# Attention scores: two heads side by side in the halves of TensorE's rows, three matmuls of 64 rows each in place of two stacked ones of 128

## The chip, the cores and the metric

The kernel runs on one core of a Trainium2 chip. The metric is the device time of one execution in microseconds (us); lower is better. Below, TensorE is PE in the rows of the profile, its weight loads are PEld, VectorE is DVE, ScalarE is ACT, GpSimd is POOL and SyncE, which issues most transfers, is SP.

## The reference

The program is one layer of a decoder trunk on a sequence of 1,024 tokens of width 1,024: a norm, a wide projection, two token mixers, their merge and an output projection, a gated MLP with a short convolution, and a final norm. The change touches only the scores of the two mixers, that is the products of queries with keys before the softmax:

```python
# differential attention: 4 heads, each with two maps c = 0, 1 of width d = 64
s = jnp.einsum('bqhcd,bshcd->bhcqs', q_blk, k, preferred_element_type=jnp.float32) * scale
logits = s - slopes[:, None, None, None] * dist.astype(jnp.float32)
p = jax.nn.softmax(logits, axis=-1)
a = p[:, :, 0] - lam * p[:, :, 1]
...
# sliding window of 128: 8 query heads of width 64, two key heads, each shared by 4 query heads
s = jnp.einsum('bnqkgd,bnskd->bnkgqs', qb, kw, preferred_element_type=jnp.float32) * (d ** -0.5)
```

Both sum over 64 elements, half of the 128 rows that the other matmuls of this kernel use.

## The kernel before

All products are made at single precision out of two parts of a shortened float format: a number x is split into a high part xh (rounded by ScalarE) and a low part xl = x - xh (by VectorE). A product of two such numbers is normally three matmuls, high by high, high by low and low by high, added up in PSUM; low by low is left out.

The stages follow each other: `project` (the wide projection; queries and keys are stored to `qd` in memory as two parts, each as 64 rows per head, two heads in 128 rows), `attention`, `rest` (gates, merge, output projection), `hidden` and `down` (the MLP).

`attention` runs six units. Units 0 to 3 are the heads of differential attention, in steps of 128 queries (`da_step`): step i has queries i*128 to i*128+127 and keys up to (i+1)*128, so widths 128 to 1,024, in pieces ("cuts") of up to 512 columns; the first step takes 256 columns. For both maps c there are scores in a tile `sc` of the pool `psS` (two buffers), one VectorE instruction that adds the bias and finds the row's extreme (line 637, called the reduction below), one exponential on ScalarE (L638); then the two maps are combined (L643), transposed on TensorE (L649), split, and multiplied with the values in `da_av` (L661 to L663). Units 4 and 5 are the key heads of the window attention, in eight steps each (`sw_step`): four query heads, 256 columns each, scores at L721, reductions at L728, transposes at L742, the product with the values at L752.

Scores before the change are made by stacking: `q_stacks` loads the high part of one head's queries into 64 rows and the low part into the other 64 rows; `k_stack` loads the same 64 rows of the keys twice, once into each half, as one tile for the high part and one for the low part. A matmul over 128 rows then gives (qh + ql) * kh at once, a second one (qh + ql) * kl. So each head and cut has two matmuls of 128 rows, with all four terms.

The work that fills gaps in the attention stage is `back_half` (the columns of the wide projection for the gates, L160 to L162, matmuls of 512 columns), dealt out over the steps by the table `HALVES`. The order of instructions on each engine is decided when the program is built: a scheduler takes instructions by priority as their inputs come due, and each engine then runs its own list strictly as listed. `high_priority`, `issue_after` and `add_manual_dep` bend that order. A pool's `bufs` says how many tiles of one tag live at once; the parts for the scores are tiles of tag "u", eleven buffers.

Of the kernel before, what the change touches and what calls it, by code (L numbers as in the profile page):

```python
# [10 lines left out]
F32 = mybir.dt.float32  # L11
F32R = mybir.dt.float32r
AF = mybir.ActivationFunctionType
ALU = mybir.AluOpType
# [3 lines left out]
P = 128  # L18
D = 1024
T = 1024  # L20
# [20 lines left out]
C_NM, C_NF, C_NO, C_CB, C_CW, C_SUB, C_QS, C_SINK, C_LAM = 0, 8, 16, 24, 68, 200, 201, 205, 213  # L41
NVEC = C_LAM + 256


class Trunk:
    def __init__(self, tc, ins, out):
        self.tc, self.nc = tc, tc.nc
        (self.xT, self.w_in, self.w_br, self.w_mix, self.w_up, self.w_dn,
         self.vecs_d, self.bias_d) = ins
        self.out = out  # L50
        self.uid = 0
        self.stores = []
        self.uw = None
        self.front = None
        self.hs, self.defer, self.late = {}, [], []

    def name(self, s):
# [430 lines left out]
    def attention(self):  # L488
        nc, tc = self.nc, self.tc
        with ExitStack() as ctx:  # L490
            e = ctx.enter_context
            self.ap = e(tc.tile_pool(name="ap", bufs=1, side="right", reuse_waits="tile"))
            self.fpool = e(tc.tile_pool(name="fyp", bufs=1, side="right", reuse_waits="tile"))
            ap = self.ap

            lt = self.tl(self.gpool, [P, 64], "g", bufs=2)
            ls = self.st.tile([P, 4], F32, name="ls")
            for c in range(2):
                a = C_LAM + 128 * c
                nc.vector.tensor_tensor(lt, self.vecs[:, a:a + 64], self.vecs[:, a + 64:a + 128], ALU.mult)  # L500
                nc.vector.tensor_reduce(ls[:, c:c + 1], lt, axis=mybir.AxisListType.X, op=ALU.add)
            nc.scalar.activation(ls[:, 2:4], ls[:, 0:2], AF.Exp)
            self.neglam = self.cp.tile([P, 1], F32, name="neglam")
            nc.vector.tensor_tensor(self.neglam, ls[:, 3:4], ls[:, 2:3], ALU.subtract)
            nc.vector.tensor_scalar(self.neglam, self.neglam, LAM_INIT, None, ALU.subtract)
            self.nsink = self.cp.tile([P, 8], F32, name="nsink")
            nc.vector.tensor_scalar(self.nsink, self.vecs[:, C_SINK:C_SINK + 8], -1.0, None, ALU.mult)
            self.subw = self.cp.tile([P, 1], F32, name="subw")
            nc.vector.tensor_scalar(self.subw, self.vecs[:, C_SUB:C_SUB + 1], 1.0 - LAM_INIT, None, ALU.mult)

            self.bias = ap.tile([P, T + 256], F32, name="bias")
            nc.sync.dma_start(self.bias, self.bias_d)

            later = []
            st = self.q_stacks(0), self.kv_stacks(0)
            for b in self.back[0][0]:
                self.back_half(*b)
            for u in range(6):
                if st is None:
                    st = self.q_stacks(u), self.kv_stacks(u)  # L520
                if u < 4:
                    self.v_parts(u)
                elif u == 4:
                    self.sw_v(self.v32(17))
                y = self.tl(self.fpool, [P, T], "y", bufs=2) if u < 4 else None
                aT = None
                for i in range(NB):
                    if u < 4:
                        if i == 0:
                            self.s0 = self.tl(self.st, [P, NB], "s0", bufs=2)  # L530
                        if i % 2 == 0:
                            aT = self.da_at(i // 2)
                        self.da_step(u, i, st, aT)
                        if i % 2 == 1:
                            self.da_av(u, i // 2, aT, y)
                    else:
                        self.sw_step(u - 4, i, st)
                    for b in self.back[u + 1][i]:
                        self.back_half(*b)
                    self.flush(1)  # L540
                    if later:
                        later.pop(0)()
                st = None
                if u < 4:
                    later = self.da_norm(u, y)
            self.flush(0)
# [17 lines left out]

    def q_stacks(self, u):

        r = []
        for m in ((u,), (12, 13), (14, 15))[max(u - 3, 0)]:
            for c in range(2):
                a, b = slice(c * 64, c * 64 + 64), slice(64 - c * 64, 128 - c * 64)  # L570
                s = self.tl(self.ap, [P, T], "u", F32R, bufs=11)
                for part, to in enumerate((a, b)):
                    self.nc.sync.dma_start(s[to].bitcast(F32), self.qd[m, part, a])
                r.append(s)
        return r

    def k_stack(self, m, c):
# [7 lines left out]
        return r  # L585

    def kv_stacks(self, u):
        return [self.k_stack(4 + u, c) for c in range(2)] if u < 4 else self.k_stack(16, u - 4)

    def v32(self, m):  # L590
        v = self.tl(self.fpool, [P, T], "f", bufs=2)
# [27 lines left out]
    def da_step(self, h, i, st, aT):  # L619
        nc, ap = self.nc, self.ap  # L620
        q, k = st
        slope = 4.0 ** -(h + 1)
        w = (i + 1) * P

        lo = P if w == 640 else 0
        cuts = ((0, 256),) if i == 0 else ((0, w),) if w <= H2 else ((0, H2 - lo), (H2 - lo, w))
        pr = []
        for c in range(2):
            sc = self.tl(self.psS, [P, T], "sc")
            qs = q[c][:, i * P:(i + 1) * P]  # L630
            for part in range(2):
                for n0, n1 in cuts:
                    nc.tensor.matmul(sc[:, lo + n0:lo + n1], qs, k[c][part][:, n0:n1], start=part == 0, stop=part == 1)  # L633
            L = self.tl(ap, [P, T], "L", bufs=4)
            s = self.tl(self.st, [P, 4], "sm", bufs=8)
            o = 896 - i * P
            nc.vector.tensor_tensor_reduce(L[:, :w], sc[:, lo:lo + w], self.bias[:, o:o + w], slope, 3e38, ALU.add, ALU.min, s[:, 0:1])  # L637
            nc.scalar.activation(L[:, :w], L[:, :w], AF.Exp, bias=s[:, 0:1], scale=-1.0, accum_out=s[:, 1:2] if c else self.s0[:, i:i + 1])  # L638
            pr.append(L)

        nc.vector.reciprocal(s[:, 2:3], s[:, 1:2])
        nc.vector.tensor_scalar(s[:, 3:4], self.s0[:, i:i + 1], s[:, 2:3], self.neglam, ALU.mult, ALU.mult)
        nc.vector.scalar_tensor_tensor(pr[0][:, :w], pr[1][:, :w], s[:, 3:4], pr[0][:, :w], ALU.mult, ALU.add)  # L643
        qo = (i % 2) * P
        for j0 in range(0, i + 1, 4):
            nj = min(4, i + 1 - j0)
            ps = self.tl(self.psT, [P, 4, P], "t")
            for j in range(nj):
                nc.tensor.transpose(ps[:, j, :], pr[0][:, (j0 + j) * P:(j0 + j + 1) * P], self.ident)  # L649
            hi, lo = aT[j0 // 4, 0], aT[j0 // 4, 1]  # L650
            nc.scalar.copy(hi[:, :nj, qo:qo + P], ps[:, :nj, :])
            nc.vector.tensor_tensor(lo[:, :nj, qo:qo + P], ps[:, :nj, :], hi[:, :nj, qo:qo + P].bitcast(F32), ALU.subtract)
# [57 lines left out]
    def sw_step(self, g, n, st):  # L710
        nc, ap = self.nc, self.ap
        q, k = st
        k0 = max(n - 1, 0) * P
        w = P if n == 0 else 256
        bo = T + (P if n == 0 else 0)
        sc = self.tl(self.psS, [P, 4, 256], "sc")
        s = self.tl(self.st, [P, 4, 4], "sw", bufs=4)
        L = self.tl(ap, [P, 4, 256], "L", bufs=4)
        for h in range(4):
            for part in range(2):  # L720
                nc.tensor.matmul(sc[:, h, :], q[h][:, n * P:(n + 1) * P], k[part][:, k0:k0 + 256], start=part == 0, stop=part == 1)  # L721


        a, at, we = (0, w, w + 1) if n == 0 else (1, 0, w)
        nc.gpsimd.tensor_copy(L[:, :, at:at + 1], self.nsink[:, 4 * g:4 * g + 4].unsqueeze(2))
        for h in range(4):
            slope, ns = 2.0 ** -(4 * g + h + 1), self.nsink[:, 4 * g + h:4 * g + h + 1]
            nc.vector.tensor_tensor_reduce(L[:, h, a:w], sc[:, h, a:w], self.bias[:, bo + a:bo + w], slope, ns, ALU.add, ALU.min, s[:, 0, h:h + 1])  # L728
        for h in range(4):
            nc.scalar.activation(L[:, h, :we], L[:, h, :we], AF.Exp, bias=s[:, 0, h:h + 1], scale=-1.0, accum_out=s[:, 2, h:h + 1])  # L730
# [5 lines left out]
        po = self.tl(self.psT, [P, H2], "t")  # L736
        nblk = w // P
        parts = []
        for b in range(nblk):
# [4 lines left out]
            hi, lo = pt[:, 0], pt[:, 1]  # L744
# [7 lines left out]
                nc.tensor.matmul(po, va, pt, start=b == 0 and m == 0, stop=b == nblk - 1 and m == 1)  # L752
        t = self.tl(self.gpool, [P, 4, P], "g", bufs=2)[0:64]
        nc.scalar.copy(t, po[64:128].rearrange("p (h q) -> p h q", h=4))
        pv = po[0:64].rearrange("p (c e q) -> p c e q", c=2, e=2)
        tv = t.rearrange("p (c e) q -> p c e q", e=2)
        y = self.tl(ap, [P, 2, P], "ys", bufs=3)
        for e in range(2):
            nc.vector.tensor_tensor(y[64 * e:64 * e + 64], pv[:, :, e], tv[:, :, e], ALU.add)
# [548 lines left out]
```

## Time and profile before

| | us |
|---|---|
| median of 3 runs | 1328.85 (1328.23 to 1329.53) |
| the profiled execution's own time | 1328.35 |
| its span, first to last instruction | 1326.6 |
| scores of differential attention on PE (L633) | 253.7 to 387.3, 192 matmuls |
| scores of window attention on PE (L721) | 387.7 to 471.0, 128 matmuls |
| granted TensorE clock | 0.998 |

Columns of the rows by group: line, engine, operation, tiles written and read, rows*columns of the array, shape, count | busy us, mean ns of one | idle time of the engine just before them and what ended it. A matmul's time in a row is from its start to its end, and successive matmuls overlap; the distance from one start to the next is what a matmul costs in a stream. Rows by time have the start, the length, the engine, the line and the operation; "x6" is six in a row, and the length then runs from the first start to the last end. Rows of stretches have, for each engine, the busy us and in brackets the number of instructions.

### The profile page before, as it was taken

To read this page: it belongs to the slowest core of one execution; us is meant where nothing else is said; L and a number is where in the kernel's file an instruction comes from. 1 tells how busy PE (TensorE), PEld (TensorE's weight loads), DVE (VectorE), ACT (ScalarE), POOL (GpSimd) and SP (SyncE) were. 2 spreads that over 40 slices of the span, in tenths; PEclk is the share of its full clock that TensorE was granted. 3 is DMA by queue.
4 is the path that set the end of the run, shared out by engine and by line. 5 is a ranking of instruction groups with operands and counts; after the bars stand their busy time and mean duration, and the time that the engine had idled before them with its cause. 6 is when DMAs were issued, how large, how long until landed. Compare 5 with 4: busy or idle time off the path is not lost. (4 is left out here: it accounts for less than half of the span.)

```text
span 1326.6 us, 17120 instructions
## 1 busy us (share of the span) xinstructions
PE 1309.5 (99%) x6210; PEld 1088.9 (82%) x6210; DVE 1057.2 (80%) x1456; ACT 621.1 (47%) x967; POOL 480.4 (36%) x364
## 2 busy tenths in 40 slices
PE   9999999999999999999999999999999999999997
PEld 7888888888888878888888888888888787888886
DVE  8846775289888976445669999999999998896865
ACT  8532232276667764333444433343343435554543
POOL 0446652000111015651435657766767641000002
PEclk9999999999999999999999999999999999999999
DMA  7334443976554235334423435564536226963534
GB/s 261 120 143 158 145 148 127 265 183 184 150 129 136 85 132 211 136 111 159 133 105 132 174 123 149 141 210 135 157 138 167 77 86 234 339 198 117 166 98 147
DMA packets 71588, 205.96 MB, mean 155 GB/s; under 512 B 8016, under 2 KB 15824, under 8 KB 71376
## 3 DMA queue, kind: packets, MB, share of 16 engines
q1 hardware_dynamic: 57472, 176.03, 39.6%
q0 software_dynamic: 2304, 11.54, 4.6%
q10 hardware_dynamic: 11728, 17.31, 3.6%
q8 instruction: 49, 0.80, 0.3%
q14 instruction: 35, 0.29, 0.1%
HBM read 156.08 MB, written 71.83 MB: 172 GB/s over the span
## 5 line engine op out<-in xcount | busy, mean ns | idle before, releaser
L141 DVE TENSOR_TENSOR wl<-raw,wh 128x1024 fp32r<-128x1024 f32 (+2 forms) x85 | 97.3, 1146 | 56.4 <-ACT wh L139 46.8
L139 ACT CAST wh<-raw 128x1024 fp32r<-128x1024 f32 (+2 forms) x85 | 74.2, 874 | 113.3 <-PE y L1121 49.4
L1051 POOL TENSOR_TENSOR us<-us,rstd 128x1024 f32<-128x1024 f32 x42 | 93.1, 2277 | 51.8 <-DVE us L466 32.7
L1065 ACT ACTIVATE c<-us,vecs 128x1024 f32<-128x1024 f32 x44 | 54.8, 1247 | 115.5 <-POOL us L1051 109.9
L120 DVE TENSOR_TENSOR sl<-sf,sh 128x1024 fp32r<-128x1024 f32 x62 | 92.7, 1496 | 15.6 <-ACT sh L118 15.6
L118 ACT CAST sh<-sf 128x1024 fp32r<-128x1024 f32 x62 | 64.7, 1045 | 83.8 <-PE t L901 44.0
L104 POOL TENSOR_TENSOR sf<-rv 128x512 f32<-128x512 f32 x30 | 58.0, 1935 | 116.6 <-DVE sl L120 51.1
L177 POOL TENSOR_TENSOR rs<-ms,mhalf 128x8 f32<-128x8 f32 (+2 forms) x9 | 13.3, 1474 | 234.4 <-DVE ms L175 228.3
L1121 PE MATMUL y<-h,wh 128*128 128x512 f32 (+1 forms) x324 | 95.1, 377 | 0.0
L1121 PE MATMUL d<-h,wh 128*128 128x512 f32 x264 | 81.3, 389 | 0.0
L1068 DVE SCALAR_TENSOR_TENSOR c<-us,vecs,c 128x1024 f32<-128x1024 f32 x44 | 75.4, 1746 | 0.1
L160 PE MATMUL g<-xh,wh 128*128 128x512 f32 x176 | 70.9, 403 | 1.5 <-ACT g L562 1.5
L161 PE MATMUL g<-xl,wh 128*128 128x512 f32 x176 | 70.3, 400 | 0.0
L162 PE MATMUL g<-xh,wl 128*128 128x512 f32 x176 | 70.3, 399 | 0.0
L120 DVE TENSOR_TENSOR wl<-raw,wh 128x1024 fp32r<-128x1024 f32 (+1 forms) x32 | 69.1, 2159 | 0.1
L1121 PEld LDWEIGHTS y<-h,wh 128*128 128x128 f32 x324 | 59.4, 188 | 11.0
L106 POOL TENSOR_TENSOR sf<-raw,rv 128x512 f32<-128x512 f32 x30 | 54.0, 1798 | 36.8 <-DVE sl L120 36.8
L1067 DVE SCALAR_TENSOR_TENSOR c<-us,vecs,c 128x1024 f32<-128x1024 f32 x44 | 63.0, 1464 | 1.6 <-ACT c L1065 1.5
L637 DVE CUSTOM_DVE_ANT_0 L<-sc,bias 128x128 f32<-128x128 f32 (+7 forms) x64 | 47.7, 751 | 17.0 <-PE sc L633 13.7
L616 POOL MEMSET aT<- 128x128 f32 x32 | 6.2, 206 | 151.7 <-PE t L662 98.0
L1121 PE MATMUL y<-h,wl 128*128 128x512 f32 (+1 forms) x162 | 60.9, 376 | 0.0
L638 ACT ACTIVATE L<-L,sm 128x128 f32<-128x128 f32 (+7 forms) x64 | 49.6, 778 | 20.0 <-DVE sm L637 17.3
(394 smaller groups left out, 4156.1 us busy)
## 6 DMA issues: line engine op xcount, KB each, us to landing
u<-qd SPq DMA_DIRECT2D x72, 256.0 KB, 6.3
raw<-in_w_up SPq DMA_DIRECT2D x23, 512.0 KB, 5.0
raw<-in_w_in SPq DMA_DIRECT2D x22, 512.0 KB, 3.8
hd<-c SPq DMA_DIRECT2D x22, 512.0 KB, 2.6
sdP<-in_w_down POOLq DMA_DIRECT2D x16, 704.0 KB, 9.0
rv<-in_w_up SPq DMA_DIRECT2D x21, 512.0 KB, 4.6
hc<-hd SPq DMA_DIRECT2D x33, 256.0 KB, 5.0
gr<-gd SPq DMA_DIRECT2D x16, 512.0 KB, 3.5
```

Of the source, the lines that this page charges most:

```text
L104: tt(sa[:, 0], v[:, 0], v[:, 1], ALU.add)
L118: cast = nc.scalar.copy(hi, src)
L120: low = nc.vector.tensor_tensor(lo, src, hi.bitcast(F32), ALU.subtract)
L139: self.hi = nc.scalar.copy(wh, raw)
L141: self.lo = (eng or nc.vector).tensor_tensor(wl, raw, wh.bitcast(F32), ALU.subtract)
L160: nc.tensor.matmul(ps, wh[:, kc + o, :], ah, start=first and n == 0, stop=False)
L161: nc.tensor.matmul(ps, wh[:, kc + o, :], al, start=False, stop=False)
L162: nc.tensor.matmul(ps, wl[:, kc + o, :], ah, start=False, stop=last and n == len(kcs) - 1)
L1051: i = (nc.vector if m % NF == 0 else nc.gpsimd).tensor_tensor(us[:, 2:], us[:, 2:], self.rstd, ALU.mult)
L1067: nc.vector.scalar_tensor_tensor(c, us[:, 1:T + 1], cw[1], c, ALU.mult, ALU.add)
L1068: nc.vector.scalar_tensor_tensor(c, us[:, 0:T], cw[0], c, ALU.mult, ALU.add)
L1121: nc.tensor.matmul(ps, v[:, k - k0, :], x, start=start and k == i == 0, stop=k == HK - 1 and i == 2, skip_group_check=True)
```

## The change

For each cut, the scores of two heads are now made by six matmuls of 64 rows: three terms (qh*kh, ql*kh, qh*kl; ql*kl is left out, as in the other products) for each of two heads, one in rows 0 to 63 of the array and the other in rows 64 to 127, alternating, each head to its own tile or half of a tile. In differential attention the two are the maps c = 0, 1 of a head; in window attention they are neighbouring query heads, whose places in the score tile are rearranged for it (`HEADS`, and the sinks with them). Since a part of 128 rows holds two heads as it lies in `qd`, tiles are now loaded as they are (`parts_of`), 128 rows by two transfers; for differential attention the keys are no longer loaded twice. Window attention still loads its key head twice, into both halves.

The score matmuls are built at a priority of 300, and the first one of a step in differential attention gets an added wait on the last reduction of the step before (`self.red`).

```diff
+TERMS = ((0, 0), (1, 0), (0, 1))
+HEADS = (0, 2, 1, 3)
+PRIO = 300
...
+        return [self.parts_of(m) for m in ((u,), (12, 13), (14, 15))[max(u - 3, 0)]]
+
+    def parts_of(self, m):
+
         r = []
-        for m in ((u,), (12, 13), (14, 15))[max(u - 3, 0)]:
+        for part in range(2):
+            t = self.tl(self.ap, [P, T], "u", F32R, bufs=11)
             for c in range(2):
-                a, b = slice(c * 64, c * 64 + 64), slice(64 - c * 64, 128 - c * 64)
-                s = self.tl(self.ap, [P, T], "u", F32R, bufs=11)
-                for part, to in enumerate((a, b)):
-                    self.nc.sync.dma_start(s[to].bitcast(F32), self.qd[m, part, a])
-                r.append(s)
+                a = slice(64 * c, 64 * c + 64)
+                self.nc.sync.dma_start(t[a].bitcast(F32), self.qd[m, part, a])
+            r.append(t)
         return r
...
-        return [self.k_stack(4 + u, c) for c in range(2)] if u < 4 else self.k_stack(16, u - 4)
+        return self.parts_of(4 + u) if u < 4 else self.k_stack(16, u - 4)
...
-        for c in range(2):
-            sc = self.tl(self.psS, [P, T], "sc")
-            qs = q[c][:, i * P:(i + 1) * P]
-            for part in range(2):
-                for n0, n1 in cuts:
-                    nc.tensor.matmul(sc[:, lo + n0:lo + n1], qs, k[c][part][:, n0:n1], start=part == 0, stop=part == 1)
+        scs = [self.tl(self.psS, [P, T], "sc") for _ in range(2)]
+        for n0, n1 in cuts:
+            for n, c in [(n, c) for n in range(3) for c in range(2)]:
+                with self.tc.high_priority(PRIO):
+                    (qp, kp), sc, r = TERMS[n], scs[c], slice(64 * c, 64 * c + 64)
+                    mm = nc.tensor.matmul(sc[:, lo + n0:lo + n1], q[0][qp][r, i * P:(i + 1) * P], k[kp][r, n0:n1], start=n == 0, stop=n == 2)
+                    if n0 == n == c == 0 and self.red is not None:
+                        self.tc.add_manual_dep(mm.ins, self.red.ins.name, mybir.DependencyInfo(mybir.DependencyClass.Sync, mybir.DependencyReason.DATA), reason="both banks")
+        for c, sc in enumerate(scs):
...
-            nc.vector.tensor_tensor_reduce(L[:, :w], sc[:, lo:lo + w], self.bias[:, o:o + w], slope, 3e38, ALU.add, ALU.min, s[:, 0:1])
+            self.red = nc.vector.tensor_tensor_reduce(L[:, :w], sc[:, lo:lo + w], self.bias[:, o:o + w], slope, 3e38, ALU.add, ALU.min, s[:, 0:1])
...
-        for h in range(4):
-            for part in range(2):
-                nc.tensor.matmul(sc[:, h, :], q[h][:, n * P:(n + 1) * P], k[part][:, k0:k0 + 256], start=part == 0, stop=part == 1)
-
+        for c in range(2):
+            for i, (qp, kp) in enumerate(TERMS):
+                for e in range(2):
+                    r = slice(64 * e, 64 * e + 64)
+                    with self.tc.high_priority(PRIO):
+                        nc.tensor.matmul(sc[:, 2 * e + c, :], q[c][qp][r, n * P:(n + 1) * P], k[kp][r, k0:k0 + 256], start=i == 0, stop=i == 2)
...
-            slope, ns = 2.0 ** -(4 * g + h + 1), self.nsink[:, 4 * g + h:4 * g + h + 1]
+            slope, ns = 2.0 ** -(4 * g + HEADS[h] + 1), self.nsink[:, 4 * g + h:4 * g + h + 1]
...
-        pv = po[0:64].rearrange("p (c e q) -> p c e q", c=2, e=2)
-        tv = t.rearrange("p (c e) q -> p c e q", e=2)
+        pv = po[0:64].rearrange("p (e c q) -> p c e q", c=2, e=2)
+        tv = t.rearrange("p (e c) q -> p c e q", e=2)
```

The sinks are negated into the new order by the same single VectorE instruction as before (L507). In the order of the built program the 480 new score matmuls stand on PE in 50 unbroken stretches, with other matmuls between them (four short ones in the first step, then 31 of one step of differential attention each, 14 of one step of window attention, and one of two such steps); before, the 320 stood in 109 stretches, in part mixed one by one with others.

More of the change, by code (lines that the diff above doesn't have):

```diff
@@ L53, in __init__ @@
         self.uw = None
-        self.front = None
+        self.front = self.red = None
         self.hs, self.defer, self.late = {}, [], []
@@ L506, in attention @@
             self.nsink = self.cp.tile([P, 8], F32, name="nsink")
-            nc.vector.tensor_scalar(self.nsink, self.vecs[:, C_SINK:C_SINK + 8], -1.0, None, ALU.mult)
+            nc.vector.tensor_scalar(self.nsink.rearrange("p (g e c) -> p g c e", g=2, e=2), self.vecs[:, C_SINK:C_SINK + 8].rearrange("p (g c e) -> p g c e", g=2, c=2),
+                                    -1.0, None, ALU.mult)
             self.subw = self.cp.tile([P, 1], F32, name="subw")
```

## The prediction

> **What bounds the kernel now.** I read the page first, then the busy time by stretches of the attention stage, then the groups by shape, then single instructions in order of time, and last the waits.
>
> ```profile
> span 1326.6 us, 17120 instructions
> PE 1309.5 (99%) x6210; PEld 1088.9 (82%) x6210; DVE 1057.2 (80%) x1456; ACT 621.1 (47%) x967; POOL 480.4 (36%) x364
> ```
>
> ```profile
> 250.00:390.00 140.00, 139.92 (x860) 121.34 (x859) 112.61 (x295) 90.97 (x212) 10.64 (x32) 1.00 0.63 169
> 390.00:475.00 85.00, 83.81 (x512) 71.98 (x511) 78.08 (x264) 62.67 (x176) 8.24 (x31) 1.00 0.40 118
> ```
>
> The columns after the length are PE, PEld, DVE, ACT and POOL, then the granted clock and the DMA share. PE is the bound of the whole program and of both halves of attention: 139.92 of 140 us in differential attention, 83.81 of 85 in window attention. VectorE is next, with 27 us free in the first and 7 us in the second. So a microsecond of score matmuls more or less is a microsecond of the time, as long as VectorE keeps up.
>
> What one score matmul costs is its distance to the next, not its length. The groups give the counts:
>
> ```profile
> L1121 PE MATMUL d<-h,wh 128*128 128x512 f32 x264 | 81.3, 389 | 0.0
> ...
> L633 PE MATMUL sc<-u,u 128*128 128x512 f32 x80 | 27.7, 410 | 0.0
> ...
> L662 PE MATMUL t<-aT,v 128*128 128x256 f32 x80 | 22.6, 282 | 0.0
> L649 PE MATMUL t<-ident,L 128*128 128x128 f32 x144 | 22.2, 274 | 0.1
> L721 PE MATMUL sc<-u,u 128*128 128x256 f32 x128 | 21.1, 291 | 0.0
> L633 PE MATMUL sc<-u,u 128*128 128x256 f32 x64 | 16.8, 299 | 0.0
> ...
> L633 PE MATMUL sc<-u,u 128*128 128x384 f32 x48 | 15.3, 352 | 0.0
> ...
> L168 PE MATMUL t<-ones,sq 128*128 128x1 f32 x64 | 7.6, 240 | 0.0
> ```
>
> The distances come from stretches of one kind, first from the chain of waits, then from the order of time:
>
> ```profile
> 1133.72 60.09 PE d L1121 x264
> ```
>
> ```profile
> 302.46 0.64 PE L633 MATMUL sc<-u,u 128*128 128x384 f32 x3
> 302.94 0.28 PE L661 MATMUL t<-aT,v 128*128 128x256 f32 x1
> ```
>
> ```profile
> 390.70 0.88 PE L721 MATMUL sc<-u,u 128*128 128x256 f32 x6
> 391.42 0.93 PE L649 MATMUL t<-ident,L 128*128 128x128 f32 x7
> 392.10 1.32 PE L721 MATMUL sc<-u,u 128*128 128x256 f32 x9
> ```
>
> ```profile
> 1291.57 0.95 PE L168 MATMUL d<-ones,c 128*128 128x1 f32 x8
> ```
>
> With 512 columns a matmul costs 60.09/264 = 0.227 us. With 256 it costs (0.88-0.28)/5 = 0.12 (six reach from the first start to the last end, and one is 0.28 long, L662). The three from 302.46 to 302.94 are the cuts 384, 256, 384 of one step, so 384 columns cost (0.48-0.12)/2 = 0.18. With 128 columns it is (0.93-0.27)/6 = 0.11, and with a single column (0.95-0.24)/7 = 0.10 (0.24 is the length of one such, L168). The last two matter most: below 256 columns the price no longer follows the columns. Something of 0.11 us per matmul, its own weight load or its issue, becomes the floor.
>
> So the scores cost PE now 80*0.227 + 48*0.18 + 64*0.12 = 34.5 us in differential attention and 128*0.12 = 15.4 in window attention, 49.9 in all.
>
> **The change, part by part.** *Matmuls.* Four matmuls per pair of heads and cut become six: 80, 48, 64 and 128 become 120, 72, 96 and 192. If two neighbours in opposite halves of the rows run at once, that is 60, 36, 48 and 96 pairs. What a pair costs no row of before shows, since every matmul there has 128 rows. Bounds:
> - Lowest: a pair costs what one matmul does, its two weight loads side by side too. 60*0.227 + 36*0.18 + 48*0.12 = 25.9, and 96*0.12 = 11.5: 37.4, a gain of 12.5 us (8.6 and 3.9).
> - Middle: the streams overlap, but a pair still has two loads and two issues, at 0.11 each: no pair is under 0.22. 60*0.227 + 36*0.22 + 48*0.22 = 32.1, and 96*0.22 = 21.1: 53.2, a loss of 3.3 (a gain of 2.4 in differential, a loss of 5.7 in window attention).
> - Highest: no overlap at all, 2*37.4 = 74.8, a loss of 24.9.
>
> I take the middle. The nearest row is the one with a single column: there is nothing to stream, and the matmul still takes 0.10 with its load. Two matmuls bring two such floors unless the two halves have a path each. Pairs of 512 columns hide two floors, the 144 pairs of 256 (all of window attention among them) cannot.
>
> *Switching.* PE goes from matmuls of 128 rows to pairs of 64 and back 50 times, 100 switches. No row shows one. The free end: 391.42 above is a change from float32r products to float32 transposes, and the seven of them fill 0.68 us until 392.10, no more than seven in a stream. The dear end: the array empties first. A matmul's length beyond its distance is the depth that would be exposed: 389-227 ns for 512 columns (L1121) and 282-120 for 256 (L662) both give 0.162 us; with a weight load (0.11) that can't be made ahead, 0.27. So 0 to 27 us for 100. I take 0.05 each, 5 us, nearer to the switch that is seen than to one that only might be. The Trainium skill, "TensorEngine Tiling (Array Packing)", section "Tiling Modes", says that changing the tiling mode drains TensorE; no row here bears it out or denies it, and by that rule alone this term would be some 16 us.
>
> *The added wait.* The first score matmul of a step now waits for both reductions of the step before. Behind it in PE's list stand the rest of its group, then transposes, products with the values and gate matmuls; ScalarE's copies and VectorE's subtractions wait for those. And both reductions now wait for the scores of both maps.
>
> ```profile
> PEld sc L633 <- DVE sm L637: 1.6, 7, 0.3
> ...
> PEld sc L721 <- DMA u<-qd: 0.3, 1, 0.3
> ```
>
> ```profile
> DVE L L637 <- PE sc L633: 13.7, 7, 7.2
> ```
>
> ```profile
> sum 140.00, DVE 48.16; mean DVE 12.04
> ```
>
> Such waits cost PE 1.6 us before, and VectorE waited 13.7 us for scores. The last row is line 637's own busy time on VectorE from 250 to 390 us: 64 reductions in 48.16 us, 0.75 each. If each of 31 steps waited for one reduction more, 23 us; if the order puts enough other matmuls between, nothing. The built order has 5 to 36 matmuls between two groups of differential attention after the first step, at the fewest five gate matmuls, 1.1 us, so I take 0 and keep a few microseconds for the range. VectorE's extra wait for a longer group is covered by its 27 us free.
>
> *Loads.* 16 of these 72 transfers go (keys of four heads, two parts, two halves):
>
> ```profile
> u<-qd SPq DMA_DIRECT2D x72, 256.0 KB, 6.3
> ```
>
> PE waited for this kind 0.3 us, for one transfer of window attention, whose loads stay. So 0; the cover is the gate matmuls. Four tiles a head of eleven let the next head load sooner, which nobody waits for.
>
> *Smaller.* The sinks are still one instruction. The window's rearranged adds and exponentials keep number and size: 0.
>
> **Sum.** 3.3 + 5 = +8.3 us on the profiled execution's 1328.35 (span 1326.6 and 1.75 around it) gives 1336.7; the median lies 0.5 above that execution, so 1337.
>
> **The rivals.**
> - *Side by side in full, switches cheap (faster).* The pair costs as one: -12.5, with 0 to 5 us of switches and waits given back, 1316 to 1324. For it: the two halves share neither rows nor tiles. Against it: the floor of 0.10 with one column. It decides where a pair of 256 columns costs under about 0.17 (144 such pairs move 1.4 us per 0.01, those of 384 give at most 36*0.04 = 1.4, and 8.3 have to go). VectorE would not stop it: window attention would shed 3.9 of PE's 83.81 against VectorE's 78.08. The Trainium skill, "TensorE: Matmul & The Clock Gate", "Part 3: Packing small matmuls — row/col tiling", speaks for it: matmuls in different row groups start about 4 ns apart. No row of before shows such a pair.
> - *Side by side, but the array drains at each switch.* -12.5 + 100*0.162 = +3.7, 1332; with the weight load exposed too, +14.5, 1343. This is the tiling page's rule as a mechanism here.
> - *Floor and drain together.* 3.3 + 16 to 27: 1348 to 1359.
> - *No overlap.* The change doesn't do what it says, two heads merely follow each other: +24.9 and more, 1353 to 1380.
>
> **How the numbers follow.** Forecast (0.22 a pair, cheap to half-price switches, 1331 to 1346): 0.38. Fully side by side with cheap switches: 0.31. Side by side with drains: 0.14, of which 0.02 faster, 0.04 same. Floor and drain: 0.10. No overlap: 0.07. A difference of 0.2% (2.7 us) is about what a measurement of this kernel can tell from none. Faster 0.33; same 0.06, with 0.02 of the forecast; slower 0.61. The range leaves out no overlap, most of floor and drain, and the best corner of the fast rival: 1315 to 1350.
>
> **What would show it.** In the profile after: rows "64*128" for the scores; the distance from the first half of a pair to the first half of the next, for 256 columns 0.22 by the forecast and 0.12 by the fast rival, for 512 columns 0.23 by both and 0.45 without overlap. For switches, the distance from the last 64-row matmul to the next 128-row one, and from the last of 128 to the first of 64, against 0.12 to 0.23. For the added wait, idle time of PEld before the scores that ends with the reduction, 1.6 us before. PE's busy share would stay near 99% in all cases, so the stretch's length has to be read: first score to the last was 253.7 to 471.0. I am wrong if pairs of 256 columns run well under 0.2, or if a switch costs more than the depth.

## The result, and the profile after

The changed kernel takes 1345.36 us (median of 4 runs, 1344.99 to 1346.89); the kernel before took 1329.19 in the same comparison. The ratio is 1.0124, with a 95% interval of 1.0109 to 1.0139: 16.2 us slower. The direction was forecast and the time lies in the range, but the forecast of +8 us is half of what came.

The page of the changed kernel, and its busy time in the two stretches shown before (PE, PEld, DVE, ACT, POOL, granted clock, DMA share):

```profile
span 1345.1 us, 17412 instructions
PE 1319.7 (98%) x6370; PEld 1077.5 (80%) x6370; DVE 1058.1 (79%) x1456; ACT 621.3 (46%) x967; POOL 477.0 (35%) x364
```

```profile
250.00:390.00 140.00, 133.64 (x869) 102.62 (x867) 103.83 (x268) 81.57 (x193) 10.79 (x31) 1.00 0.47 132
390.00:475.00 85.00, 81.03 (x560) 62.55 (x560) 78.89 (x259) 62.30 (x172) 6.63 (x30) 1.00 0.37 110
```

PE no longer fills differential attention: 133.64 of 140 us, where it was 139.92. Where the time came from can be bounded by one instruction, the first matmul of the merge after attention. Before, then after:

```profile
500.98 0.39 PE L160 MATMUL sc<-yh,wh 128*128 128x512 f32 x1
```

```profile
518.18 0.39 PE L165 MATMUL sc<-yh,wh 128*128 128x512 f32 x1
```

17.2 of the 18.5 us between the two profiled spans arise in the attention stage. (This profiled execution, 1346.89 us, was the slowest of the four.) The stage from 250 us up to that instruction, before, then after:

```profile
250.00:500.98 250.98, 248.85 (x1483) 213.21 (x1482) 208.42 (x591) 170.92 (x418) 23.90 (x67) 1.00 0.54 153
```

```profile
250.00:518.18 268.18, 257.81 (x1642) 199.86 (x1641) 214.78 (x592) 173.51 (x420) 22.77 (x67) 1.00 0.44 130
```

So PE is busy 9.0 us longer, and idle for 10.4 us where it was idle for 2.1. (The split is not exact: busy time counts the whole length of the last matmul before each idle gap, which is 0.16 us more than its distance.)

What a pair costs and what a switch costs stand in one stretch of window attention, in order of time:

```profile
431.31 0.40 PE L166 MATMUL g<-xl,wh 128*128 128x512 f32 x1
431.64 0.98 PE L736 MATMUL sc<-u,u 64*128 64x256 f32 x12
432.55 1.09 PE L756 MATMUL t<-ident,L 128*128 128x128 f32 x8
```

Twelve matmuls of 256 columns reach from the first start to the last end in 0.98 us. Less the length of one (0.28) that is 0.70 for the five distances between six pairs: four of 0.12, and the first longer by 0.10. One after the other they would need 11*0.12 = 1.3. So the halves run side by side, weight loads included, and a pair costs what one matmul of 128 rows did.

Then the switches. The first score comes 0.33 us after a 512-column matmul, which otherwise costs 0.23: 0.10 lost. The second pair comes 0.10 late, because its weights were not loaded ahead. The last pair starts at 431.64 + 0.70 = 432.34, the transposes at 432.55 rather than 0.12 later: 0.09 lost. Over the stretches that no idle time touches, the trace has on average 0.10 on entering, 0.105 before the second pair, 0.10 on leaving and 0.08 at the second matmul after. Together that is 0.38 us a stretch, some 0.19 a switch.

What PE's weight loads (first block) and PE itself (second block) waited for, in differential attention:

```profile
PEld sc L642 <- DVE sm L649: 6.1, 15, 1.0
PEld sc L642 <- issue: 3.9, 13, 0.4
PEld t L661 <- issue: 3.8, 6, 1.5
PEld t L673 <- DVE aT L664: 3.4, 6, 1.4
```

```profile
PE t L661 <- DVE L L655: 1.6, 3, 1.1
PE t L673 <- DVE aT L664: 1.6, 2, 1.0
PE t L188 <- DVE y L704: 1.5, 2, 0.8
PE sc L642 <- DVE sm L649: 1.1, 2, 0.5
```

The weight loads' idle time before the scores that ends with the reduction went from 1.6 to 6.1 us, but that is not all waiting: 13 other times the loads stood idle for 0.3 us before the scores with nothing to wait for ("issue"), as the run with the switch alone will show too, and the 15 waits are 0.4 us each, hardly more. PE itself idled 1.1 us before the scores. Most of its idle time stands before the transposes and the products with the values behind them (L661, L673, L188), which wait for VectorE; before the change no wait of PE itself is listed from 250 to 400 us.

### The profile page after: what moved, and what is told of

It reads as the page before. It is cut to its first block, busy times and chain, and to the rows that moved or that the text cites. A ratio compares the mean times of both kernels' runs of the same rounds, so it can differ in the third digit from the quotient of the medians.

```text
span 1345.1 us, 17412 instructions
## 1 busy us (share of the span) xinstructions
PE 1319.7 (98%) x6370; PEld 1077.5 (80%) x6370; DVE 1058.1 (79%) x1456; ACT 621.3 (46%) x967; POOL 477.0 (35%) x364
## 5 line engine op out<-in xcount | busy, mean ns | idle before, releaser
L146 DVE TENSOR_TENSOR wl<-raw,wh 128x1024 fp32r<-128x1024 f32 (+2 forms) x85 | 92.6, 1090 | 56.2 <-ACT wh L144 46.5
L649 DVE CUSTOM_DVE_ANT_0 L<-sc,bias 128x128 f32<-128x128 f32 (+7 forms) x64 | 47.6, 752 | 13.7 <-PE sc L642 10.4
```

Of the source, the lines that this page charges most:

```text
L146: self.lo = (eng or nc.vector).tensor_tensor(wl, raw, wh.bitcast(F32), ALU.subtract)
```

## Experiments

Theory: pairs do run side by side (about -12 us), but every stretch of 64-row matmuls costs 0.38 us by its two switches (50 of them, +19), and the grouped scores with the added wait cost some 10 us more. Rivals: the switches cost nothing and all is waiting; or the pairs gain nothing.

**The switch alone.** Of the kernel before, one of four score matmuls per cut is put on 64 rows, in place and unpaired.

```diff
-                    nc.tensor.matmul(sc[:, lo + n0:lo + n1], qs, k[c][part][:, n0:n1], start=part == 0, stop=part == 1)
+                    r = slice(0, 64) if part and not c else slice(0, 128)
+                    nc.tensor.matmul(sc[:, lo + n0:lo + n1], qs[r], k[c][part][r, n0:n1], start=part == 0, stop=part == 1)
```

> The kernel before, with one of its four score matmuls per cut of differential attention (the low part of the keys with the first map) on 64 rows instead of 128, which leaves out ql*kl of that map. Number, order and columns of the matmuls stay as before; nothing is paired and no wait is added. 38 stretches of 64-row matmuls, one or two long. If the switch itself is dear: 38 times 0.28 (no second pair) to 0.38, +11 to +14, 1340 to 1343. If the loss comes from the added wait and the grouping: no change, 1329.

Measured 1342.41 us, ratio 1.0103 [1.0088, 1.0118]: +13.4, 0.35 for each of 38 stretches. In the profiled execution the granted clock was 0.51 for 3.4 us (303.1 to 306.5), which costs up to 1.7 us; without that the price is 0.31. One of the 38 in order of time; the first row is a 128-row and a 64-row matmul of 256 columns:

```profile
330.93 0.59 PE L634 MATMUL sc<-u,u 128*128 128x256 f32 x2
331.45 0.50 PE L161 MATMUL g<-xl,wh 128*128 128x512 f32 x1
331.78 0.40 PE L634 MATMUL sc<-u,u 128*128 128x256 f32 x2
```

The two take 0.52 until the gate matmul, in place of 0.24, and that one takes 0.33 in place of 0.23: 0.38. What the weight loads of these scores waited for shows no other engine of weight; their idle time has no releaser ("issue"):

```profile
  issue: 7.3, 29
  DVE ms L684: 0.5, 2
```

The switch is dear by itself, with no pair, no added wait and the same number of matmuls.

**The order and the wait alone.** The kernel before with its 128-row matmuls, but the change's priority, the maps in turn, and the added wait.

```diff
+        scs = [self.tl(self.psS, [P, T], "sc") for _ in range(2)]
+        with self.tc.high_priority(300):
+            for part, n0, n1, c in [(part, n0, n1, c) for part in range(2) for n0, n1 in cuts for c in range(2)]:
+                mm = nc.tensor.matmul(scs[c][:, lo + n0:lo + n1], q[c][:, i * P:(i + 1) * P], k[c][part][:, n0:n1], start=part == 0, stop=part == 1)
...
+                    self.tc.add_manual_dep(mm.ins, self.red.ins.name, ...)
```

> The kernel before with its own stacked matmuls of 128 rows, all 192 of them in differential attention, but with the priority of 300, the two maps of a step in turn and the added wait: the change's order and wait without its halves. No switches, no pairs. If the waits of 8 to 12 us in differential attention come from the grouping and the added wait: 1337 to 1341. If they come with the halves: 1329.

Measured 1340.47 us, ratio 1.0082 [1.0066, 1.0097]: +10.5. In the two stretches its PE is idle 7.9 us (1.74 and 6.11), against 10.3 (6.36 and 3.97) in the changed kernel and 1.3 before, and among what its weight loads wait for are the same things:

```profile
250.00:390.00 140.00, 138.26 (x829) 118.75 (x828) 104.64 (x273) 83.06 (x195) 10.39 (x31) 1.00 0.61 162
390.00:475.00 85.00, 78.89 (x465) 66.49 (x466) 74.71 (x246) 59.52 (x166) 6.31 (x29) 0.96 0.39 112
```

```profile
PEld sc L634 <- DVE sm L641: 2.6, 6, 1.3
...
PEld t L665 <- ACT aT L655: 2.0, 4, 0.9
```

Before, TensorE made scores of the one map while VectorE reduced the other. Once both maps' scores are one block that waits for both reductions, the two engines take turns, and the work between the blocks doesn't always fill the turn. The halves are not needed for that loss.

The 10.5 us are not all waiting, though. The second row has a granted clock of 0.96: from 391.7 to 395.1 us and from 402.0 to 405.4 it was half (0.51 and 0.50). Two groups of eight score matmuls, one just before the first of these times and one within it (in brackets, the idle time before the group and what ended it):

```profile
387.38 1.67 PE L634 MATMUL sc<-u,u 128*128 128x512 f32 x8
391.66 3.31 PE L634 MATMUL sc<-u,u 128*128 128x512 f32 x8 [1.11 <-DVE sm L641]
```

That is 1.6 us there and at most 1.7 in the other, some 3 in this execution; the changed kernel's trace has a clock of 1.00 in the whole stage. Over whole executions the granted clock hardly differs (0.995 to 0.996 here and in the runs of the kernel before beside them), so how much of the 10.5 is the clock stays open: the order and the wait cost some 7 to 10.5 us.

**One stage at a time.** Window attention alone, and differential attention alone, with the other stage's lines as before:

> 64-row pairs in window attention alone; differential attention as before, so no added wait. 17 stretches. By the two terms seen in the traces (a pair costs one matmul, a stretch 0.38 us by its switches): -3.9 + 17*0.38 = +2.6, 1331.5. If switches were free: 1325. If most of the loss were the added wait, which is only in differential attention: at or below 1329.

Measured 1331.75 us, ratio 1.0028 [1.0018, 1.0037]: +3.2, where pairs and switches gave +2.6.

> 64-row pairs in differential attention alone; window attention as before. 35 stretches. -8.6 + 35*0.38 = +4.7 by pairs and switches alone, 1333.7; what it is above that is waiting of TensorE for VectorE and ScalarE, some 8 us in the changed kernel's trace, so 1341. If switches alone explain the loss: 1334.

Measured 1345.42 us, ratio 1.0127 [1.0111, 1.0144]: +16.9. Pairs and switches give +4.7, so some 12 are left; of these 9.7 show in the trace as further idle time of PE in the stage (11.8 against 2.1 us). The stage without the added wait follows the two terms within a microsecond; the stage with it lies 12 above them. The two runs add up to +20.1, where both stages changed at once cost +16.2, so the terms are not independent.

**Without the added wait.** The line with `add_manual_dep` goes.

```diff
-                    if n0 == n == c == 0 and self.red is not None:
-                        self.tc.add_manual_dep(mm.ins, self.red.ins.name, ...)
```

> The changed kernel without the added wait on the second reduction of the step before. The built order then has 75 stretches instead of 50, since the first head's scores go ahead of the second's. If the added wait is what TensorE idles for: some 8 us back, less 25*0.38 = 9.5 for the further stretches, 1343 to 1349. If the added wait costs nothing: 1345 + 9.5 = 1355. If switches cost nothing: 1337.

Measured 1365.46 us, ratio 1.0277 [1.0260, 1.0294]: 20 us worse than the changed kernel, outside all I had written. The waits did go (PE is idle 1.6 us in the stage, against 10.4), but so did the pairs: the first map's scores now stand ahead of the second's in a stretch of their own.

```profile
319.19 1.67 PE L642 MATMUL sc<-u,u 64*128 64x512 f32 x6
320.78 0.38 PE L673 MATMUL t<-aT,v 128*128 128x256 f32 x1
```

Six matmuls take 1.59 us here; side by side they would be three distances of 0.227 and a switch. By their start times some 290 of the 480 score matmuls have no partner, against some 20 in the changed kernel. At one matmul's price for a pair and for a single, that is some 26 us more of PE; 25 further stretches (9.5) come on top, and 8.8 of idle time off. That makes 27 where 20 were measured, so one of these terms is too high, and I can't say which. I had counted stretches, and forgotten that a matmul of 64 rows alone costs as much as one of 128.

**Another order within a stretch.** In the code, three terms of the first head, then three of the second, in both kinds of attention; the line of differential attention:

```diff
-            for n, c in [(n, c) for n in range(3) for c in range(2)]:
+            for n, c in [(n, c) for c in range(2) for n in range(3)]:
```

> The changed kernel with the six matmuls of a cut in another order: three of the first head, then three of the second, so neighbours lie in the same half of the rows (only the third and fourth still differ). If the pairs run side by side, three passes become five: scores of 37.4 us at one matmul's price per pair become 62, so about +25 us, 1370. If running side by side gains nothing, the order does not matter: 1345.

Measured 1348.71 us, ratio 1.0151 [1.0134, 1.0168]: +3.3 against the changed kernel, not +25. It told nothing on whether pairs gain, since they were still pairs. In differential attention the scheduler undid most of that: with a and b for the two halves, its list on PE has a a b a b b in a step of one cut and a a b a b a b a b a b b in one of two. Window attention kept the order of the code, a a a b b b a a a b b b, and there a step takes what it takes in the changed kernel (0.98):

```profile
432.03 0.99 PE L736 MATMUL sc<-u,u 64*128 64x256 f32 x12
```

Less 0.28 for the last one's length that is 0.71, or 0.10 and five distances of 0.12: six pairs. Three of one half listed first did not keep the other half waiting, so the two halves together do not run the list strictly as it stands. Of the 3.3 us, PE's idle time in the stage has 1.6 (11.9 against 10.4); the rest I have not traced.

**More switches at the same work.** A matmul of 256 columns between the two cuts of a step, with 128 rows in one run and 64 in the other.

```diff
         for n0, n1 in cuts:
+            if n0:
+                with self.tc.high_priority(PRIO):
+                    nc.tensor.matmul(scs[0][:, lo + n0:lo + n0 + 256], q[0][0][:, i * P:(i + 1) * P], k[0][:, 0:256], start=True, stop=True)
```

> The changed kernel with one matmul of 128 rows and 256 columns more between the two cuts of a step (16 in all, its product is overwritten). It cuts 16 stretches of 64-row matmuls in two: 67 stretches instead of 50. If a stretch costs 0.38 us by its two switches (what the changed kernel's trace shows: 0.10 on entering, 0.105 before the second pair, 0.09 on leaving, 0.09 at the second matmul after): 16*0.12 + 17*0.38 = +8.4, 1353.7. If switches cost nothing and the loss is all waits: 16*0.12 = +1.9, 1347.

> The same 16 matmuls more, but of 64 rows, so no stretch is cut (51 stretches). Both theories: 16*0.12 or a little more, +2 to +3, 1347 to 1348. It is the measure for the run with 128 rows.

Measured 1349.07, ratio 1.0151 [1.0136, 1.0166], and 1349.44, ratio 1.0154 [1.0139, 1.0169]. No difference: in the total time the further switches cost nothing (though both runs lie some 2 us above what I expected of free ones). On PE they are there, with 128 rows:

```profile
309.64 0.96 PE L645 MATMUL sc<-u,u 64*128 64x512 f32 x6
310.53 0.38 PE L641 MATMUL sc<-u,u 128*128 128x256 f32 x1
310.85 0.62 PE L645 MATMUL sc<-u,u 64*128 64x256 f32 x6
```

0.32 us from the added matmul to the next scores where 0.12 is the price. But PE is idle for less of the stage up to the merge. With 128 rows, then with 64:

```profile
250.00:520.86 270.86, 267.02 (x1659) 202.64 (x1657) 214.39 (x594) 175.18 (x421) 23.72 (x67) 1.00 0.44 129
```

```profile
250.00:520.67 270.67, 261.64 (x1661) 203.49 (x1660) 215.18 (x595) 175.21 (x421) 24.36 (x67) 1.00 0.45 129
```

PE is busy 5.4 us longer with the further switches, near the 6.5 of 17*0.38, and idle for 3.8 us where it is idle for 9.0 with 64 rows. So it looks as if a switch is paid out of the wait where PE waits anyway, and this pair of runs can't price it in the total. The built orders also differ between the variants, which I can't separate from it.

**A smaller dose.** The kernel before, with one pair of 64 rows in place of the two matmuls with the low part of the keys, in steps 5 to 7 only.

```diff
+        half = i >= 5
...
+                r = slice(64 * c, 64 * c + 64) if part and half else slice(0, 128)
```

> The kernel before, stacked operands and all, but in steps 5 to 7 of each head of differential attention the two matmuls with the low part of the keys are made as one pair of 64 rows (ql*kl left out), all of a step's in one stretch of four, with the added wait there. 12 stretches. Gain: one pass of each cut, (0.35 + 0.41 + 0.45)*4 = 4.8 us; switches 12*0.38 = 4.6. 1328 to 1330 by both terms; 1324 if switches were free; over 1331 if the added wait costs.

Measured 1337.22 us, ratio 1.0067 [1.0052, 1.0082]: +8.7. By the two terms gain and switches cancel. What is left goes with the grouping and the added wait of these twelve steps, the ones with the longest reductions: in the trace PE is idle for 7.6 us of the stage, against 2.1 before, and up to 1.7 us more went at half clock (398.8 to 402.2). No version that I could see from here beats the kernel before: by this estimate, without any waits the pairs of differential attention would still lose 4.7 us.

**Priority 0.**

> The changed kernel with priority 0 in place of 300 for the score matmuls, the added wait kept. The built order has 107 stretches instead of 50. By 0.38 us a stretch: +21.7, less the waits that go (up to 10): 1357 to 1367. If a stretch costs little: at or below 1345.

Measured 1373.34 us, ratio 1.0327 [1.0310, 1.0344]: 107 stretches instead of 50, +28 us against the changed kernel, more than forecast. One reason for the excess shows in the granted clock (the last column but two):

```profile
300.00:350.00 50.00, 49.51 (x300) 37.32 (x299) 34.14 (x88) 26.58 (x62) 4.92 (x15) 0.97 0.33 97
350.00:400.00 50.00, 48.88 (x292) 36.21 (x289) 34.44 (x87) 27.44 (x64) 4.67 (x13) 0.93 0.31 90
400.00:450.00 50.00, 46.15 (x295) 35.80 (x294) 39.95 (x118) 29.90 (x79) 3.70 (x13) 0.90 0.26 72
```

What the three rows lack of a full clock is up to 10 us of work.

## Why the prediction was right or wrong

By its own steps:

- *PE is the bound, and scores lie on the path.* Right before the change. After it PE idles 6 us in differential attention, so the bound is in part the turn-taking with VectorE.
- *A pair costs 0.22 us, two floors of 0.11.* Wrong, and the largest miss. A pair of 256 columns costs 0.12, the lowest of my three bounds; the term is -12.5, not +3.3. I had taken the floor seen with one column for a cost per matmul on PE as a whole; it is one per path, and the two halves have a path each. What the Trainium skill says in "TensorE: Matmul & The Clock Gate", "Part 3: Packing small matmuls — row/col tiling", that matmuls in different row groups run at once, the trace bears out: six pairs in 0.98 us.
- *A switch costs 0.05 us, 5 in all.* Wrong, and nearly as large a miss. It costs 0.19 (0.16 to 0.18 by the run with the switch alone), between the two dear values I had worked out (0.162 from the exposed depth, 0.27 with a load), so 50*0.38 = 19. I had put it near the free change from products to transposes, which keeps all 128 rows; that row was the wrong neighbour. The rule of "TensorEngine Tiling (Array Packing)", "Tiling Modes", in the Trainium skill, that a change of mode drains TensorE, agrees with the trace (0.10 us lost on entering, 0.09 on leaving). The rest of the price is the second matmul after each switch, 0.08 to 0.10 late; behind the entry its weights are not loaded ahead.
- *The added wait costs 0, with 23 at most.* Wrong: 7 to 10.5 us when order and wait are made alone. I had counted matmuls between the groups, five at the fewest (1.1 us), against one reduction of 0.75; but a group waits for two, and neither starts before the scores of both maps are done.
- *Loads and smaller edits, 0.* Nothing in the waits of the trace after points to them: none on a transfer of "u" is among the longest.

The terms as measured: -12.5 + 19 + 7 to 10.5 = +13.5 to +17, against 16.2. The first two are from traces, the last from a run of its own; that they add up is no proof of each, since switches and waits overlap, as the run with further switches shows. The rival that came nearest was "side by side, but the array drains at each switch", with the load exposed: +14.5, worked out to 1343. It held 0.14 between its two prices, too little, and it lacked the waits. That my +8.3 had the right sign was luck: two errors of opposite sign (15.8 on the pairs, 14 on the switches) nearly cancelled, and the wait was what remained.

## What to carry to other kernels

Packing two 64-row matmuls side by side pays in full here, but each visit to that mode costs some 0.38 us, so a visit has to save well more than that: a step that saves 0.24 to 0.45 us can't carry a visit of its own. Before grouping work to save such visits, ask what the grouping makes wait: two engines that overlapped piece by piece take turns once the pieces are one block. And a matmul that is split in two must find its partner in the same stretch, or the split has doubled it.

## What the runs showed of the hardware that I had not expected

- The two halves take their matmuls independently of the order in the list: three of one half, then three of the other, still ran as pairs (0.71 us from the first of twelve to the last, 256 columns each, as with the halves in turn).
- Weight loads of the two halves run at once too: pairs of 256 columns follow each other at 0.12 us, though a matmul of 128 rows with a single column comes no faster than 0.10.
- TensorE's granted clock fell to half for short times within the attention stage: 3.4 us once in the runs with the switch alone and with the smaller dose, 3.4 us twice in the run with the order and the wait alone, and 20 us in all with priority 0 (0.90 over the 50 us from 400 to 450). In the traces of the kernel before and of the changed kernel it was 1.00 in the whole stage. What brings it on no run here shows: PE was idle for 7 to 8 us of the stage in three of these four runs, but for 2 in the one with the switch alone, and for 10 in the changed kernel, whose clock did not fall.
